# Differential heads: the inverse square root of the output norm moves from VectorE to GpSimd

## The chip, the cores and the metric

The kernel runs as one program on one core of a Trainium2 chip. The metric is the device time of an execution in microseconds (us); the time before is the median of three runs. A profile is one further execution with the hardware profiler on. Engines are named TensorE (PE in the rows; PEld its weight loads), VectorE (DVE), ScalarE (ACT), GpSimd (POOL) and SyncE (SP), which here issues the DMAs.

## What is computed

The model is two layers of a diffusion backbone over 1152 tokens (128 context, 1024 latent). The change lies in the second layer, in its eight differential-attention heads. For one head, with its own learned gate z and a scalar lam:

```python
s = jnp.einsum('bhiqd,bhikd->bhiqk', qb, k).astype(jnp.float32) * scale
p = jax.nn.softmax(s, axis=-1)
attn = p[:, :, 0] - lam * p[:, :, 1]
oc = jnp.einsum('bhqk,bhkv->bhqv', attn.astype(v.dtype), v)
...
oc = rmsnorm(oc, subln_g) * (1 - lam_init)   # per token, over the head's 128 values
out = jnp.concatenate([oc * jax.nn.silu(zc), od * jax.nn.silu(zd)], axis=-1) @ w_out
```

The norm needs one inverse square root for each token and head: 1152 for a head, which lie as 128 partitions by 9 columns.

## The kernel before

Tokens are cut into nine blocks of 128. Every large product is split into three half-precision products (high x high, high x low, low x high), so each operand lives as a pair (tile names ending in `hl`: high and low).

`odd` runs the eight heads one after the other (`diff_head`, heads 0 to 7 in the text), and after them eight window blocks of the other attention (`win_block`). For each block of queries a head computes two score maps of 1152 columns into `psS` (two PSUM buffers of three banks, so the next map waits until the last reader of the one before is done), VectorE takes the maximum (`sms`, L1290), ScalarE the exponential and its sum (L1292), VectorE combines the two maps into `p` (L1302 and L1303), ScalarE rounds `p` to half precision and GpSimd subtracts to get the low half (`phl`, L1304 and L1305), SyncE transposes it into `PT`, and about three blocks later TensorE multiplies it with V (`diff_pv`). ScalarE copies that result to `og` and sums its squares into `oss` (`diff_out`).

Between the scores TensorE works on the projections for the next heads, handed out in small pieces by a filler (`F.take`): `qk_block` for keys and queries and `v_block` for values. A projection's chunk of 384 columns goes to one of two PSUM buffers `psmm`; in `qk_block` it is read by ScalarE (`raw`, L1169) and VectorE (`q` times the cosine, L1175), then VectorE shuffles `raw` into `sw` (L1179), GpSimd multiplies by the sine and adds (L1180, L1181), and at the end ScalarE and GpSimd split `q` into `qhl` (L1187, L1188), which DMAs lay out as K or Q. TensorE can start the chunk after next only when both readers of a buffer are done. Weights are split into `whl` by ScalarE and VectorE (L322, L323).

When a head's last block is out, `diff_out` makes `oss` the mean square, `rsqrt` computes its inverse square root `orr` in integer and Newton steps, and `try_finish` multiplies `og` by it (L1249) and by the gate `zs` (L1250), splits the product into `gl` (ScalarE L509, GpSimd L510) and stores it. This falls some blocks into the next head's scores. In head 7 it falls into the first window block, where VectorE's masked reduction is L1378.

TensorE's order is that of the program. On the other engines a scheduler puts the instructions in order when the program is built, by priorities; the scores' and projections' readers have high priority, and the head's norm has not. Each engine then works its list strictly in order.

Of the kernel before, what the change touches and what calls it, by code (L numbers as in the profile page):

```python
# [10 lines left out]
F32 = mybir.dt.float32  # L11
F16 = mybir.dt.float16
I32 = mybir.dt.int32
AF = mybir.ActivationFunctionType
ALU = mybir.AluOpType
# [4 lines left out]
P = 128  # L20
# [3 lines left out]
NCH = T // P  # L24
KD = 8
WS = 64.0
IWS = 1.0 / WS
# [193 lines left out]
class Builder:  # L221
# [146 lines left out]
    def rsqrt(self, out, v, w, pool=None):  # L368

        nc = self.nc  # L370
        y = self.tl(pool or self.cm, [P, w], F32, f"rqy{w}")
        a = self.tl(pool or self.cm, [P, w], F32, f"rqa{w}")
        yi = y.bitcast(I32)
        nc.vector.tensor_scalar(yi, v.bitcast(I32), 1, None, ALU.logical_shift_right)
        nc.vector.tensor_scalar(yi, yi, -1, 0x5F3759DF, ALU.mult, ALU.add)
        for it in range(3):
            nc.vector.tensor_tensor(a, y, v, ALU.mult)
            nc.vector.scalar_tensor_tensor(a, a, -0.5, y, ALU.mult, ALU.mult)
            nc.vector.scalar_tensor_tensor(out if it == 2 else y, a, 1.5, y, ALU.add, ALU.mult)

    def rstd_stats(self, ssq, c0, c1, n):

        nc = self.nc
        m = (c1 - c0) // P
        st = self.pt("mm")
        for j in range(m):
            nc.tensor.matmul(st[:, j:j + 1], ssq[:, c0 + j * P:c0 + (j + 1) * P], self.ones[:, 0:1], start=True, stop=True)
        return self.rstd_diag(st[:, :m], m, n)
# [737 lines left out]
    def odd_setup(self):  # L1126
        nc, A = self.nc, self.A
        self.cosT = self.tl(self.rot, [P, TL], F32, "cos", 1)
        nc.sync.dma_start(self.cosT, A["cos"])
        self.sinT = self.tl(self.rot, [P, TL], F32, "sin", 1)  # L1130
        nc.sync.dma_start(self.sinT, A["sin"])
        self.mask = self.wt([P, 7, P], F32, tag="mask", bufs=1)
        nc.sync.dma_start(self.mask, A["mask"])

        lm = self.row("lam").rearrange("p (a b c) -> p a b c", a=2, b=2)
        pr = self.tl(self.rot, [P, 384], F32, "raw", 2)[:, :128].rearrange("p (a b) -> p a b", a=2)
        nc.vector.tensor_tensor(pr, lm[:, :, 0], lm[:, :, 1], ALU.mult)
        sm = self.wt([P, 4], F32, tag="lms", bufs=1)
        nc.vector.tensor_reduce(out=sm[:, 0:2], in_=pr, axis=AX.X, op=ALU.add)
        nc.scalar.activation(sm[:, 0:2], sm[:, 0:2], AF.Exp)  # L1140
        nc.vector.tensor_tensor(sm[:, 2:3], sm[:, 1:2], sm[:, 0:1], ALU.subtract)
        nc.vector.tensor_scalar(sm[:, 3:4], sm[:, 2:3], LAM_INIT, None, ALU.subtract)
        self.nlam = sm[:, 3:4]
        self.nsink = self.wt([P, 16], F32, tag="nsink", bufs=1)
        nc.vector.tensor_scalar(self.nsink, self.row("sink"), -1.0, None, ALU.mult)

# [92 lines left out]
    def try_finish(self, k):  # L1239

        if ("z", k) not in self.R or ("o", k) not in self.R:
            return
        zs, (og, r) = self.R.pop(("z", k)), self.R.pop(("o", k))
        nc = self.nc
        f = "p a b -> p (a b)"
        if r is None:
            nc.vector.scalar_tensor_tensor(og.rearrange(f), og.rearrange(f), 0.5 * IWS, zs.rearrange(f), ALU.mult, ALU.mult)
        else:
            nc.vector.tensor_tensor(og, og, r[:, :NCH].rearrange("p (a b) -> p a b", b=1).broadcast_to([P, NCH, P]), ALU.mult)  # L1249
            nc.vector.tensor_tensor(og.rearrange(f), og.rearrange(f), zs.rearrange(f), ALU.mult)  # L1250
        gl = self.wt([P, 2, NCH * P], F16, tag="gl", bufs=1)
        if k == 15:
            with self.tc.high_priority():
                self.split(gl, og.rearrange(f))
                t = self.ht()
                nc.sync.dma_start_transpose(t.rearrange("p a (c q) -> p (a c) q", q=P), gl.rearrange(f))
            self.gs[15] = t
            return
        self.split(gl, og.rearrange(f), nc.gpsimd)
        nc.sync.dma_start(self.go_dr[k], gl.rearrange(f))  # L1260
# [67 lines left out]
    def diff_out(self, po, h, b, sm, og, oss):  # L1328
        nc = self.nc
        nc.scalar.activation(og[:, b], po, AF.Copy, scale=sm[:, 6:7])  # L1330
        sq = self.wt([P, P], F32, tag="osq", bufs=1)
        nc.scalar.activation(sq, og[:, b], AF.Square, accum_out=oss[:, b:b + 1])
        if b < NCH - 1:
            return
        r = self.wt([P, 16], F32, tag="orr", bufs=2)
        nc.vector.tensor_scalar(oss[:, :NCH], oss[:, :NCH], 1.0 / 128, EPS, ALU.mult, ALU.add)
        self.rsqrt(r[:, :NCH], oss[:, :NCH], NCH)
        nc.vector.tensor_scalar(r[:, :NCH], r[:, :NCH], 0.5 * IWS, None, ALU.mult)
        del self.R["v", h]
        self.R["o", h] = (og, r)  # L1340
        self.try_finish(h)
# [310 lines left out]
```

## Time and profile before

| | |
|---|---|
| time before, median of 3 runs | 2256.24 us (2253.14 to 2256.71) |
| the profiled execution: its time, its span | 2259.94 us, 2258.0 us |
| mean granted TensorE clock | 0.957 of full speed |
| TensorE busy | 2025.2 us, 90% of the span |
| VectorE busy | 1470.4 us, 65% |
| ScalarE busy | 1223.2 us, 54% |
| GpSimd busy | 1060.9 us, 47% |
| chain that ended last, by engine | TensorE 42%, VectorE 20%, GpSimd 10%, ScalarE 9% |

The shares are means over the whole program. The last line follows the work that ended last backwards, step by step, to what released it. TensorE is busy for nine tenths of the span, so what an edit on another engine is worth shows only where TensorE waits, and these places must be looked at one by one. The eight heads lie between about 1040 and 1700 us.

### The profile page before, as it was taken

The page shows a single profiled execution, that of the slowest core. Times are in us where ns is not written, and L with a number is a line of the kernel's source. Part 1 is how long each engine was busy: PE and PEld are TensorE (multiplying, and loading weights), DVE is VectorE, ACT ScalarE, POOL GpSimd, SP SyncE. Part 2 cuts the span into 40 slices and gives each one's busy share as a digit, 9 for nine tenths or more (in the row PEclk, how much of TensorE's full clock was granted, in tenths as well). Part 3 has the DMA queues.
Part 4 walks back from the last instruction along what each step waited for, and adds up shares of the span by engine and source line. Part 5 has one row for each costly group of instructions (what it writes and reads, how often), then busy time and mean ns, then how long its engine had stood idle before and what let it go on. Part 6 is the DMA issues. An engine that isn't in the chain of part 4 may idle for free.

```text
span 2258.0 us, 49764 instructions
## 1 busy us (share of the span) xinstructions
PE 2025.2 (90%) x20258; PEld 1433.6 (63%) x20258; DVE 1470.4 (65%) x2722; ACT 1223.2 (54%) x2891; POOL 1060.9 (47%) x997
## 2 busy tenths in 40 slices
PE   5997788887989999998998999999988998998997
PEld 2654475564556655665776776776666777785566
DVE  5878988789586445575677677767765545451334
ACT  5575666566463312344655655665567867782321
POOL 1378677876675200044345345445446655661001
PEclk8998898998999999999999999999999999999999
DMA  7221513224557622035454554555456968899312
GB/s 281 72 79 48 152 58 102 75 94 122 183 202 217 164 99 88 31 132 118 95 122 108 117 123 113 112 126 115 109 123 134 175 146 160 163 176 210 139 47 84
DMA packets 435125, 283.10 MB, mean 125 GB/s; under 512 B 374448, under 2 KB 385232, under 8 KB 434896
## 3 DMA queue, kind: packets, MB, share of 16 engines
q1 hardware_dynamic: 433920, 279.34, 49.9%
q8 instruction: 158, 2.59, 0.5%
q10 hardware_dynamic: 976, 0.58, 0.1%
q14 instruction: 71, 0.58, 0.1%
HBM read 133.38 MB, written 29.05 MB: 72 GB/s over the span
## 4 chain that ended last, share of the span: by engine, by line
PE 42%; DVE 20%; POOL 10%; ACT 9%; issue 6%; DMA 5%; SPq 2%; POOLq 0%; ACTq 0%; DVEq 0%
PE psmm L329 8%; PE psmm L330 8%; PE psmm L331 8%; DVE sms L1290 3%; PE psS L1288 3%; DVE whl L323 3%; PE psm L329 2%; PE psm L330 2%; PE psm L331 2%; DVE p L1303 2%; DMA Q<-qhl 2%; ACT p L1380 1%; ACT p L1292 1%; DVE E L801 1%; PE psss L331 1%
## 5 line engine op out<-in xcount | busy, mean ns | idle before, releaser
L329 PE MATMUL psmm<-h,whl 128*128 128x384 f16 (+1 forms) x1104 | 370.2, 336 | 21.3 <-DVE q L1175 14.7
L330 PE MATMUL psmm<-h,whl 128*128 128x384 f16 (+1 forms) x1104 | 369.1, 335 | 2.3 <-DVE h L506 1.7
L331 PE MATMUL psmm<-h,whl 128*128 128x384 f16 (+1 forms) x1104 | 369.0, 335 | 0.0
L329 PE MATMUL psmm<-whl,h 128*128 128x128 f16 x1920 | 334.0, 220 | 10.1 <-DVE V L1211 10.1
L330 PE MATMUL psmm<-whl,h 128*128 128x128 f16 x1920 | 333.7, 220 | 0.0
L331 PE MATMUL psmm<-whl,h 128*128 128x128 f16 x1920 | 333.6, 220 | 0.0
L330 PEld LDWEIGHTS <-whl 128*128 128x128 f16 x2256 | 225.5, 100 | 167.9 <-issue 47.2
L331 PEld LDWEIGHTS <-whl 128*128 128x128 f16 x2256 | 225.2, 100 | 157.1 <-issue 18.9
L329 PEld LDWEIGHTS <-whl 128*128 128x128 f16 x2256 | 226.3, 100 | 147.3 <-issue 23.3
L1305 POOL TENSOR_TENSOR phl<-p,phl 128x1152 f16<-128x1152 f32 (+1 forms) x72 | 155.9, 2169 | 218.5 <-ACT phl L1304 218.5
L330 PEld LDWEIGHTS <-h 128*128 128x128 f16 x2520 | 246.7, 98 | 12.6 <-issue 10.8
L329 PEld LDWEIGHTS <-h 128*128 128x128 f16 x2520 | 246.8, 99 | 4.3 <-issue 2.6
L331 PEld LDWEIGHTS <-h 128*128 128x128 f16 x2520 | 246.6, 98 | 0.0
L323 DVE SCALAR_TENSOR_TENSOR whl<-w,whl 128x512 f16<-128x512 f32 x248 | 196.5, 811 | 67.0 <-ACT whl L322 66.0
L1290 DVE TENSOR_REDUCE sms<-psS 128x1 f32<-128x1152 f32 (+1 forms) x136 | 176.5, 1298 | 67.0 <-PE psS L1288 66.2
L1390 POOL TENSOR_TENSOR phl<-p,phl 128x1024 f16<-128x1024 f32 (+2 forms) x72 | 135.1, 1876 | 106.8 <-ACT phl L1389 85.8
L322 ACT ACTIVATE whl<-w 128x512 f16<-128x512 f32 x248 | 140.1, 609 | 78.2 <-PE psmm L331 42.2
L1288 PE MATMUL psS<-K,Q 128*128 128x512 f16 (+1 forms) x800 | 153.2, 328 | 25.1 <-DVE p L1303 19.3
L1180 POOL TENSOR_TENSOR sw<-sw,sin 128x384 f32<-128x384 f32 (+1 forms) x78 | 85.8, 1101 | 150.6 <-DVE sw L1179 127.2
L503 POOL TENSOR_TENSOR h<-mt,h 128x384 f16<-128x384 f32 (+2 forms) x32 | 28.9, 913 | 250.0 <-ACT h L502 250.0
L1288 PEld LDWEIGHTS <-Q 128*128 128x128 f16 x800 | 73.5, 99 | 94.2 <-DVE p L1303 21.9
L1292 ACT ACTIVATE psS<-psS,sms 128x1152 f32<-128x1152 f32 (+1 forms) x72 | 79.1, 1098 | 89.4 <-DVE sms L1290 88.9
(396 smaller groups left out, 5864.7 us busy)
## 6 DMA issues: line engine op xcount, KB each, us to landing
w<-in_wod SPq DMA_DIRECT2D x52, 512.0 KB, 4.0
w<-in_wev SPq DMA_DIRECT2D x40, 512.0 KB, 4.1
E<-csrow SPq DMA_DIRECT2D x36, 512.0 KB, 4.0
Q<-qhl SPq DMA_DIRECT2D x64, 288.0 KB, 4.3
go_dr<-gl SPq DMA_DIRECT2D x15, 576.0 KB, 3.9
wada<-in_w_ada SPq DMA_DIRECT2D x32, 256.0 KB, 5.8
o<-in_w_ada SPq DMA_DIRECT2D x16, 512.0 KB, 5.8
xT<-in_w_ada SPq DMA_DIRECT2D x16, 512.0 KB, 6.1
```

The lines of the kernel that those rows point to most:

```text
L322: nc.scalar.activation(hl[:, 0, a:e], w[:, a:e], AF.Copy if scale is None else AF.Identity, scale=sc)
L323: nc.vector.scalar_tensor_tensor(hl[:, 1, a:e], w[:, a:e], sc, hl[:, 0, a:e], ALU.mult, ALU.subtract)
L329: mm(out, ah, bh, start=start, stop=False)
L330: mm(out, ah, bl, start=False, stop=False)
L331: mm(out, al, bh, start=False, stop=stop)
L1180: nc.gpsimd.tensor_tensor(sw[:, o:], sw[:, o:], self.sinT[:, a:b], ALU.mult)
L1288: nc.tensor.matmul(sv[:, i, c0:c1], q[:, m, x, qs], k[:, m, o + c0:o + c1], start=x == 0, stop=x == 1)
L1290: nc.vector.tensor_reduce(out=sm[:, ms[0]:ms[-1] + 1], in_=sv, axis=AX.X, op=ALU.max, negate=True)
L1292: nc.scalar.activation(sv[:, i] if m else e, sv[:, i], AF.Exp, bias=sm[:, m:m + 1], accum_out=sm[:, 4 + m:5 + m])
L1303: nc.vector.scalar_tensor_tensor(p[0], p[1], sm[:, 2:3], p[0], ALU.mult, ALU.add)
L1305: nc.gpsimd.tensor_tensor(phl[:, w:2 * w], p[0], phl[:, :w], ALU.subtract)
L1390: nc.gpsimd.tensor_tensor(phl[:, 2 * w:4 * w], p, phl[:, :2 * w], ALU.subtract)
```

## The change

`rsqrt_pool` takes the place of `rsqrt` in `diff_out`. The two integer instructions that make the first guess stay on VectorE, as does the one that makes `oss` the mean square. The three Newton rounds run on GpSimd as thirteen `tensor_tensor` instructions on 128x9: one that multiplies the mean square by -0.5, then three rounds of four. Their constants -0.5 and 1.5 come from a tile `half`, filled once in `odd_setup`. The scale by `0.5 * IWS`, a VectorE instruction of its own before, moves into the product of `og` and `orr`.

```diff
+    def rsqrt_pool(self, out, v, w):
+        nc = self.nc
+        g = nc.gpsimd.tensor_tensor
+        y = self.tl(self.cm, [P, w], F32, f"rpy{w}")
+        a = self.tl(self.cm, [P, w], F32, f"rpa{w}")
+        yi = y.bitcast(I32)
+        nc.vector.tensor_scalar(yi, v.bitcast(I32), 1, None, ALU.logical_shift_right)
+        nc.vector.tensor_scalar(yi, yi, -1, 0x5F3759DF, ALU.mult, ALU.add)
+        g(v, v, self.half[:, 0, :w], ALU.mult)
+        for it in range(3):
+            g(a, y, y, ALU.mult)
+            g(a, a, v, ALU.mult)
+            g(a, a, self.half[:, 1, :w], ALU.add)
+            g(out if it == 2 else y, a, y, ALU.mult)
...
+        self.half = self.wt([P, 2, NCH], F32, tag="half", bufs=1)
+        for i, c in enumerate((-0.5, 1.5)):
+            nc.gpsimd.memset(self.half[:, i], c)
...
-            nc.vector.tensor_tensor(og, og, r[:, :NCH].rearrange("p (a b) -> p a b", b=1).broadcast_to([P, NCH, P]), ALU.mult)
+            nc.vector.scalar_tensor_tensor(og, og, 0.5 * IWS,
+                                           r[:, :NCH].rearrange("p (a b) -> p a b", b=1).broadcast_to([P, NCH, P]),
+                                           ALU.mult, ALU.mult)
...
-        self.rsqrt(r[:, :NCH], oss[:, :NCH], NCH)
-        nc.vector.tensor_scalar(r[:, :NCH], r[:, :NCH], 0.5 * IWS, None, ALU.mult)
+        self.rsqrt_pool(r[:, :NCH], oss[:, :NCH], NCH)
```

The scheduler makes new lists of it. TensorE's is unchanged. SyncE's differs in one place, in head 6, where a transpose of `phl` now stands behind the low half of a K store. Heads 0 to 5 change alike. A line of the new program from 380 on has a number 16 to 21 higher than its like in the old one.

VectorE at the end of head 0, before: after the reduction come the steps of the first two rounds (`rqy` and `rqa`), with a shuffle and `q` between them.

```order
L1290 TENSOR_REDUCE sms_13344<-psS_13346 128x1
L379 SCALAR_TENSOR_TENSOR rqy_1526_13246<-rqa_1527_13247,rqy_1526_13246 128x9
L377 TENSOR_TENSOR rqa_1527_13247<-rqy_1526_13246,oss_11999 128x9
L1179 STREAM_SHUFFLE sw_13368<-raw_13364 128x256
L1175 SCALAR_TENSOR_TENSOR q_1533_13297<-psmm_13305,cos_11480 128x256
...
L1338 TENSOR_SCALAR orr_13244<-orr_13244 128x9
L1249 TENSOR_TENSOR og_11998<-og_11998,orr_13244 128x1152
L1290 TENSOR_REDUCE sms_13344<-psS_13388 128x1
L1175 SCALAR_TENSOR_TENSOR q_1533_13297<-psmm_13372,cos_11480 128x384
L1179 STREAM_SHUFFLE sw_13409<-raw_13406 128x384
L1250 TENSOR_TENSOR og_11998<-og_11998,zs_12596 128x1152
```

The same place in the changed program:

```order
L1311 TENSOR_REDUCE sms_13350<-psS_13352 128x1
L1268 SCALAR_TENSOR_TENSOR og_12001<-og_12001,orr_13247 128x1152
L1194 SCALAR_TENSOR_TENSOR q_1534_13303<-psmm_13311,cos_11480 128x256
L1198 STREAM_SHUFFLE sw_13374<-raw_13370 128x256
L1271 TENSOR_TENSOR og_12001<-og_12001,zs_12599 128x1152
L1311 TENSOR_REDUCE sms_13350<-psS_13394 128x1
L1194 SCALAR_TENSOR_TENSOR q_1534_13303<-psmm_13378,cos_11480 128x384
L1198 STREAM_SHUFFLE sw_13415<-raw_13412 128x384
```

The product of `og` and `orr` now stands directly behind the reduction and ahead of `q` of 128x256, and `og` times `zs` ahead of the second reduction. On ScalarE `gl` stands accordingly ahead of the next `raw` and the next exponential, where it stood behind both.

GpSimd at the end of head 0, before:

```order
L1181 TENSOR_TENSOR q_1502_13053<-q_1502_13053,sw_13284 128x384
L1188 TENSOR_TENSOR qhl_13289<-q_1502_13053,qhl_13289 128x1280
L1305 TENSOR_TENSOR phl_13336<-p_13204,phl_13336 128x1152
L1180 TENSOR_TENSOR sw_13368<-sw_13368,sin_11482 128x256
L1181 TENSOR_TENSOR q_1533_13297<-q_1533_13297,sw_13368 128x256
L1180 TENSOR_TENSOR sw_13409<-sw_13409,sin_11482 128x384
L1181 TENSOR_TENSOR q_1533_13297<-q_1533_13297,sw_13409 128x384
L510 TENSOR_TENSOR gl_13262<-og_11998,gl_13262 128x1152
```

The same place in the changed program, from the third round on; the product with -0.5 and the first two rounds, nine rows, stand between `q` of 128x384 and the first row here:

```order
L392 TENSOR_TENSOR rpa_1528_13250<-rpy_1527_13249 128x9
L393 TENSOR_TENSOR rpa_1528_13250<-rpa_1528_13250,oss_12002 128x9
L394 TENSOR_TENSOR rpa_1528_13250<-rpa_1528_13250,half_11493 128x9
L1207 TENSOR_TENSOR qhl_13295<-q_1503_13056,qhl_13295 128x1280
L395 TENSOR_TENSOR orr_13247<-rpa_1528_13250,rpy_1527_13249 128x9
L1326 TENSOR_TENSOR phl_13342<-p_13207,phl_13342 128x1152
L1199 TENSOR_TENSOR sw_13374<-sw_13374,sin_11482 128x256
L1200 TENSOR_TENSOR q_1534_13303<-q_1534_13303,sw_13374 128x256
L526 TENSOR_TENSOR gl_13268<-og_12001,gl_13268 128x1152
```

Twelve of the thirteen instructions stand ahead of `qhl`, the last one, which writes `orr`, between `qhl` and `phl`; `gl` moved ahead of the `sw` and `q` of 128x384.

VectorE in head 7, in the first window block, before (the last removed instructions, then the masked reduction of the next block's scores, an ISA row):

```order
L1387 RECIPROCAL sms_21515<-sms_21515 128x2
L379 SCALAR_TENSOR_TENSOR orr_21489<-rqa_2288_21492,rqy_2287_21491 128x9
L1338 TENSOR_SCALAR orr_21489<-orr_21489 128x9
L1249 TENSOR_TENSOR og_20265<-og_20265,orr_21489 128x1152
L1378 ISA psS_2308_21599,sms_21597<-psS_2308_21599,mask_11484,nsink_11493 128x512
```

The same place in the changed program:

```order
L389 TENSOR_SCALAR rpy_2288_21515<-rpy_2288_21515 128x9
L1406 TENSOR_REDUCE sms_21542<-sms_21542 128x2
L1407 RECIPROCAL sms_21542<-sms_21542 128x2
L1268 SCALAR_TENSOR_TENSOR og_20286<-og_20286,orr_21513 128x1152
L1398 ISA psS_2309_21626,sms_21624<-psS_2309_21626,mask_11484,nsink_11496 128x512
```

The masked reduction keeps its place behind the `og` product, and that product now takes `orr` from GpSimd, whose thirteen instructions stand there in one piece, right ahead of a `phl` of 128x1024.

## Rows read from the trace of the kernel before

**Rows 1.** Who waited for whom, TensorE, whole run: total us, times, longest.

```profile
PE psmm L329 <- DVE q L1175: 14.7, 6, 2.4
```

**Rows 2.** Timeline, TensorE: start, duration, engine, line, [idle before, releaser].

```profile
1134.38 0.48 PE L329 MATMUL psmm<-h,whl 128*128 128x384 f16 x1 [2.44 <-DVE q L1175]
...
1143.53 1.15 PE L1288 MATMUL psS<-K,Q 128*128 128x512 f16 x6 [0.53 <-DVE p L1303]
...
1147.87 0.22 PE L1321 MATMUL psS<-V,PT 128*128 128x128 f16 x1 [0.34 <-ACT og L1330]
...
1158.06 0.22 PE L329 MATMUL psmm<-whl,h 128*128 128x128 f16 x1 [1.89 <-DVE V L1211]
...
1217.39 0.32 PE L329 MATMUL psmm<-h,whl 128*128 128x384 f16 x1 [2.45 <-DVE q L1175]
...
1490.03 0.22 PE L329 MATMUL psmm<-whl,h 128*128 128x128 f16 x1 [0.72 <-DVE V L1211]
```

**Rows 3.** Timeline, VectorE, end of head 0; the last row from head 7.

```profile
1129.05 1.35 DVE L1290 TENSOR_REDUCE sms<-psS 128x1 f32<-128x1152 f32 x1
...
1131.37 2.29 DVE L377 TENSOR_TENSOR rqa<-rqy,oss 128x9 f32<-128x9 f32 x1
...
1133.92 0.41 DVE L1175 SCALAR_TENSOR_TENSOR q<-psmm,cos 128x256 f32<-128x256 f32 x1
...
1136.31 1.36 DVE L1249 TENSOR_TENSOR og<-og,orr 128x1152 f32<-128x1152 f32 x1
...
1142.06 1.42 DVE L1303 SCALAR_TENSOR_TENSOR p<-psS,sms,p 128x1152 f32<-128x1152 f32 x1
...
1147.08 1.23 DVE L323 SCALAR_TENSOR_TENSOR whl<-w,whl 128x512 f16<-128x512 f32 x1
...
1700.42 0.17 DVE L377 TENSOR_TENSOR rqa<-rqy,oss 128x9 f32<-128x9 f32 x1
```

**Rows 4.** Timeline, GpSimd, end of head 0; the last row from head 7.

```profile
1126.30 1.01 POOL L1181 TENSOR_TENSOR q<-q,sw 128x384 f32<-128x384 f32 x1
1128.69 2.62 POOL L1188 TENSOR_TENSOR qhl<-q,qhl 128x1280 f16<-128x1280 f32 x1 [1.38 <-ACT qhl L1187]
...
1131.27 2.36 POOL L1305 TENSOR_TENSOR phl<-p,phl 128x1152 f16<-128x1152 f32 x1
...
1145.37 2.39 POOL L1305 TENSOR_TENSOR phl<-p,phl 128x1152 f16<-128x1152 f32 x1
...
1702.62 3.20 POOL L1390 TENSOR_TENSOR phl<-p,phl 128x1024 f16<-128x1024 f32 x1 [3.68 <-ACT phl L1389]
```

**Rows 5.** GpSimd groups by shape (count | busy us, mean ns), then two timeline rows.

```profile
L1305 POOL TENSOR_TENSOR phl<-p,phl 128x128 f16<-128x128 f32 x8 | 3.4, 427 | 7.8 <-ACT phl L1304 7.8
...
L944 POOL TENSOR_TENSOR ed<-V,rce 128x8 f32<-128x8 f32 x4 | 0.8, 205 | 10.6 <-DVE V L937 10.6
...
1134.09 0.72 POOL L1180 TENSOR_TENSOR sw<-sw,sin 128x256 f32<-128x256 f32 x1 [0.46 <-DVE sw L1179]
1134.89 0.74 POOL L1181 TENSOR_TENSOR q<-q,sw 128x256 f32<-128x256 f32 x1
```

**Rows 6.** Timeline, GpSimd and VectorE, first layer: handovers from one to the other.

```profile
143.28 0.67 POOL L510 TENSOR_TENSOR hb<-hst,hb 128x256 f16<-128x256 f32 x1
...
143.36 0.87 DVE L766 TENSOR_TENSOR xs<-x,dec 128x256 f32<-128x256 f32 x1 [1.14 <-POOL xshl L510]
...
154.48 0.43 DVE L766 TENSOR_TENSOR xs<-x,dec 128x256 f32<-128x256 f32 x1 [0.56 <-POOL xshl L510]
```

**Rows 7.** Timeline, ScalarE, end of head 0.

```profile
1141.18 1.16 ACT L509 ACTIVATE gl<-og 128x1152 f16<-128x1152 f32 x1 [0.89 <-DVE og L1250]
```

**Rows 8.** Timeline, TensorE, end of head 6.

```profile
1639.66 0.61 PE L1288 MATMUL psS<-K,Q 128*128 128x512 f16 x1 [5.11 <-DVE p L1303]
```

**Rows 9.** Timeline, head 7: VectorE's masked reduction; TensorE.

```profile
1703.75 0.75 DVE L1378 CUSTOM_DVE_ANT_0 psS<-psS,mask,nsink 128x512 f32<-128x512 f32 x1
...
1728.14 0.37 PE L1367 MATMUL psS<-K,Q 128*128 128x128 f16 x2 [5.75 <-DMA Q<-qhl]
```

## The prediction

> **What bounds the kernel now.** I read the waits of PE first, then, at the places where the removed instructions stand, VectorE, GpSimd and ScalarE in order of time. PE lost 14.7 us in six waits for VectorE's q L1175 [rows 1]: one in each of heads 0 to 5, and head 0 stands for them. There PE has four waits [rows 2]: 2.44 us for that q, then 0.53, 0.34 and 1.89 us, 5.2 in all, the last ending at 1158.06. After it the next wait is the next head's 2.45 us at 1217.39, 83 us after 1134.38. So what counts is when PE leaves 1158.06, and a delay before it costs nothing until the last three waits, 2.76 us together, are used up. In head 4 the last wait is 0.72 us instead of 1.89, at 1490.03 [rows 2], because PE came later; it left at the same place in the head's 83 us. So the end of that wait is set by the chain on VectorE, ScalarE and GpSimd, and PE has slack in front of it. Both must be followed.
>
> Why does VectorE let q wait? The third small instruction, L377 on 128x9, took 2.29 us (1131.37 to 1133.66) [rows 3], over the same stretch in which GpSimd ran the phl subtraction (1131.27 to 1133.63) [rows 4]. A 128x9 instruction takes 0.17 us when nothing stands in its way (at 1700.42) [rows 3]. So a VectorE instruction with two inputs in SBUF stands still while GpSimd works, if GpSimd began first. The reverse holds too: in head 7 phl 128x1024 took 3.20 us at 1702.62 [rows 4] because VectorE's og product had begun before it. This lock is what the change has to be judged by.
>
> **The change part by part.** Ten small VectorE instructions per head go (three rounds of three, and the scale by 0.5*IWS, now part of the og product, whose 1.36 us [rows 3] I leave as they are: the same elements, one more constant). Thirteen GpSimd instructions on 128x9 come; the two memsets of the constants run once, in the setup, at nothing beside the input loads; if uncovered they are two tiny instructions, under half a microsecond. Two things move with them. The og product now waits for GpSimd's last instruction, orr, and all that stands behind it on VectorE waits too, q 128x256 first. And qhl and phl on GpSimd stand behind the chain.
>
> **Price of a link.** No 128x9 instruction of GpSimd is in the trace; 128x8 takes 0.205 us [rows 5]. A GpSimd instruction that needs the one before it starts 0.08 us after its end (1134.09 + 0.72 to 1134.89) [rows 5]. So a link costs 0.28. Bounds: below, VectorE's own 0.17 with no gap; above, the 128x128 form, 0.43 [rows 5], with the gap, 0.51. I take 0.28, since 8 elements are next to 9.
>
> **Head 0, GpSimd.** It is free of q at 1127.31 (1126.30 + 1.01). Twelve links, of which the second does not need the first: 12 x 0.205 + 10 x 0.08 = 3.26, to 1130.6. Then qhl, 2.62, to 1133.2; orr, 0.2, to 1133.3; phl, 2.36, to 1135.65 [rows 4]. In the kernel before, qhl started at 1128.69, since it waits for ScalarE, so part of the chain fills idle time.
>
> **Head 0, who gets the lock.** When orr ends, phl is already queued behind it and VectorE has yet to see the semaphore. The trace has this race: at 143.28 GpSimd went straight on to hb, VectorE's product, released by the instruction before hb, was issued at 143.36 and took 0.87; where GpSimd went on to something tiny the same product took 0.43 [rows 6]. So phl wins, and og runs after it. L377 ended 0.03 after phl with 0.17 of its own, so the lock comes free about 0.14 before GpSimd's end: og runs from 1135.5 to 1136.9, and q 128x256 (0.41, starting 0.08 before og's end) ends at 1137.2. Before it ended at 1134.33 [rows 3]. **PE resumes 2.86 us later** and has 2.76 of slack: +0.1.
>
> **Head 0, the VectorE chain.** Its reduction ends at 1130.40 (1129.05 + 1.35); then it stands until 1135.5, and og is over at 1136.9, where before the removed instructions, with q among them, put og at 1136.31 to 1137.67 [rows 3]. Behind q come a shuffle (estimate 0.4, as q on as many elements), og times zs (as og, 1.36) and a reduction (1.35), each starting 0.08 before its forerunner ends: done at 1140.0. On ScalarE gl (1.16) [rows 7] starts when og times zs ends, at 1138.8, and now stands ahead of raw (estimate 0.4) and of the exponential (estimate 1.2, as gl on as many elements), which ends at 1141.5. The tiny sms instruction, with two SBUF inputs, then meets GpSimd's gl subtraction (as phl, 2.36), which now comes earlier: behind sw and q (0.72 and 0.74 [rows 5], from 1138.6) it runs from 1140.1 to 1142.5. So p starts at 1142.55 instead of 1142.06 [rows 3]: +0.5. But the whl of 1147.08 stood still for 0.54 of its 1.23, because phl ran until 1147.76 (1145.37 + 2.39) [rows 3, 4]; it now starts at 1147.6, and phl, which as before waits for gl and for p's copy on ScalarE, is over. The half microsecond is given back; the chain reaches 1158.06 as before. **Heads 0 to 5: +0.1 each, +0.6.** From here each 0.1 us on the chain is 0.1 us per head, both ways, because both paths end together.
>
> **Head 6.** Here the p for which PE waits 5.11 us at 1639.66 [rows 8] has og, og times zs and seven removed instructions shortly ahead of it on VectorE. In the new order the p before it stands behind the waiting og but og and the small ones are then gone from in front of this one. Bounds: 0, if that evens out, and +3.2, the price of head 7. I take +1.0.
>
> **Head 7.** GpSimd's first rounds start when VectorE's second integer instruction is done, about 1700.4 (L377 follows it at 1700.42). The twelve links left then give 12 x 0.205 + 11 x 0.08 = 3.3: orr ends at 1703.75. Then phl 128x1024 (2.13: 3.20 less the 1.07 it stood still) holds the lock until 1705.7; og to 1707.05; the masked reduction starts at 1707.0 instead of 1703.75 [rows 9]. That reduction's successors lead through a shuffle, q, qhl and the Q transfers to PE's 5.75 us wait at 1728.14 [rows 9], where nothing gives it back: **+3.2**.
>
> Sum: 0.6 + 1.0 + 3.2 = +4.8 us. The profiled execution's own time is 2259.94 (span 2258.0 and 1.94 around it), which would become 2264.7; it lies 3.7 above the median 2256.24, so the median becomes **2261.0**. A measurement of this kernel tells 0.2% (4.5 us) from no change; the forecast stands just beyond that.
>
> **The rivals.** *GpSimd is twice as slow.* If each link takes twice VectorE's 0.17, 0.34 and the gap 0.08, the chain in head 0 takes 12 x 0.34 + 10 x 0.08 = 4.9 instead of 3.26: +1.7 in each of heads 0 to 5 (10.2), head 6 +1.5, head 7 +4.9: +16.6, 2273. Against it: the 0.205 of rows 5. The Trainium skill, GPSIMD Engine Reference, section Engine selection, speaks for it and against the whole change: elementwise work with two inputs belongs on VectorE, GpSimd being about twice as slow. By that page's ratio the time would be this rival's; its figures are for 2048 elements, and no run here shows them.
>
> *Faster.* The links run back to back at 0.17: the chain takes 2.0 instead of 3.26, and with both paths of heads 0 to 5 earlier by 1.25 they gain 1.15 each (-6.9); head 6 0, head 7 +2.0: -4.9, 2251. It turns to a gain below about 0.22 a link. For it: the links are tiny and the engine's own. Against: each waits for the one before, and the 0.08 gap is in the trace.
>
> *Head 6 and 7 absorbed.* Their delays fall where later waits take them up: +0.6, 2257. For it: PE waits often after 1640. Against: those waits hang on the same chain.
>
> *VectorE wins the lock at orr.* Then og runs at 1133.35, phl behind it, q ends only 0.7 later; p comes about 0.6 earlier than in the forecast, though og times zs now meets phl: -0.5 in six heads, head 7 +1.5 instead of 3.2, head 6 +1: about -0.5, 2256. Against: rows 6.
>
> **Chances.** Forecast 0.50 (a link of 0.25 to 0.31 moves it from +1 to +9, so 0.27 slower and 0.23 the same), twice as slow 0.18, faster 0.12, absorbed 0.12, lock won 0.08. Faster by over 0.2%: 0.13; within: 0.40; slower: 0.47. The range holds all from the faster rival to the slow one's 2273: 2250 to 2273; the forecast's own is 2257 to 2265.
>
> **What would show it.** GpSimd's 128x9 rows at 0.2 us with 0.08 between; VectorE's og row in heads 0 to 5 taking about 3.5 us (the rest of phl and its own 1.36) after an idle of 3.0; PE's wait for q at about 5.3 instead of 2.44, and the 0.53, 0.34 and 1.89 gone; head 7's Q wait later by 3. I am wrong if og takes 1.36 there, if links cost over 0.35, or if some later wait in a head's 83 us opens up.

## The result, and the profile after

The changed kernel takes 2269.43 us, median of 12 runs (2264.0 to 2275.53), against 2256.0 for the kernel before (12 runs). The ratio is 1.0051, 95% interval 1.0040 to 1.0062: **+11.5 us** (9.0 to 14.0). Five later runs of it gave 1.0048 (1.0035 to 1.0062), +10.8. The forecast was slower, +4.8, 2261.0; the time lies in the range, but the sum is short by more than half.

The steps of the forecast in head 0 can be read in the new trace. First the chain on GpSimd in head 0, by its timeline:

```profile
1126.15 0.20 POOL L392 TENSOR_TENSOR rpa<-rpy 128x9 f32<-128x9 f32 x1
1126.43 0.20 POOL L393 TENSOR_TENSOR rpa<-rpa,oss 128x9 f32<-128x9 f32 x1
...
1129.12 2.61 POOL L1207 TENSOR_TENSOR qhl<-q,qhl 128x1280 f16<-128x1280 f32 x1
1131.69 0.20 POOL L395 TENSOR_TENSOR orr<-rpa,rpy 128x9 f32<-128x9 f32 x1
1131.85 2.36 POOL L1326 TENSOR_TENSOR phl<-p,phl 128x1152 f16<-128x1152 f32 x1
```

A link takes 0.20 us and the next starts 0.28 after it, as forecast from [rows 5]. The chain, then qhl, then orr, then phl stand in the order that was forecast. VectorE's timeline in the same place:

```profile
1127.75 1.35 DVE L1311 TENSOR_REDUCE sms<-psS 128x1 f32<-128x1152 f32 x1
1131.92 3.50 DVE L1268 SCALAR_TENSOR_TENSOR og<-og,orr 128x1152 f32<-128x1152 f32 x1 [2.83 <-POOL orr L395]
1135.35 0.41 DVE L1194 SCALAR_TENSOR_TENSOR q<-psmm,cos 128x256 f32<-128x256 f32 x1
```

The og product waits 2.83 us for orr and then takes 3.50 where it took 1.36 [rows 3], since phl (1131.85 to 1134.21) has the lock. The q eviction stands behind it. TensorE's waits in all, and its timeline at the four places that matter:

```profile
PE psmm L329 <- DVE q L1194: 31.0, 6, 5.2
```

```profile
1135.81 0.48 PE L329 MATMUL psmm<-h,whl 128*128 128x384 f16 x1 [5.16 <-DVE q L1194]
...
1630.77 2.08 PE L1309 MATMUL psS<-K,Q 128*128 128x512 f16 x6 [6.57 <-ACT og L1351]
...
1682.01 0.58 PE L1387 MATMUL psS<-K,Q 128*128 128x128 f16 x4 [5.05 <-DVE p L1324]
...
1735.24 0.37 PE L1387 MATMUL psS<-K,Q 128*128 128x128 f16 x2 [5.73 <-DMA Q<-qhl]
```

The waits for q go from 14.7 [rows 1] to 31.0 us, six times 5.2, and the waits of 0.53, 0.34 and 1.89 that followed in head 0 [rows 2] are gone: one long wait in place of four short ones in that head. The row at 1682.01 answers to nothing that the prediction read. It is the first score product of the window blocks; in the kernel before it waited 1.77 us for og, and the next wait was 0.95 us for p:

```profile
1678.87 0.38 PE L1367 MATMUL psS<-K,Q 128*128 128x128 f16 x4 [1.77 <-ACT og L1330]
...
1682.16 0.22 PE L1321 MATMUL pssm<-V,PT 128*128 128x128 f16 x1 [0.95 <-DVE p L1303]
```

To find the loss I cut both traces at the first instruction of the head's norm (`oss` on VectorE, 128x9), which stands in every kernel, and at TensorE's first long wait for Q behind head 7 [rows 9]. The stretches in us, each start being a row of the timeline (before 1125.29, 1619.59, 1696.56, 1728.14; after 1124.00, 1618.75, 1700.45, 1735.24):

| stretch | before | after | after, other run |
|---|---|---|---|
| oss of head 0 to oss of head 6 | 494.30 | 494.75 | 495.09 |
| oss of head 6 to oss of head 7 | 76.97 | 81.70 | 81.77 |
| oss of head 7 to the end of the Q wait | 31.58 | 34.79 | 34.83 |
| from there to the end of the span | 529.86 | 526.96 | 529.54 |

Heads 0 to 5 lose 0.5 to 0.8 us (forecast 0.6), head 7 loses 3.2 (forecast 3.2). Between head 6 and head 7 it is 4.7 to 4.8 where 1.0 was forecast. That is the surprise.

### The profile page after: what moved, and what is told of

Its sections match the earlier page's. It is cut to its first block, busy times and chain, and to the rows that moved or that the text cites. A ratio compares the mean times of both kernels' runs of the same rounds, so it can differ in the third digit from the quotient of the medians.

```text
span 2262.2 us, 49786 instructions
## 1 busy us (share of the span) xinstructions
PE 2020.7 (89%) x20258; PEld 1435.0 (63%) x20258; DVE 1445.2 (64%) x2642; ACT 1222.2 (54%) x2891; POOL 1082.5 (48%) x1103
## 5 line engine op out<-in xcount | busy, mean ns | idle before, releaser
L331 PEld LDWEIGHTS <-whl 128*128 128x128 f16 x2256 | 225.5, 100 | 157.6 <-issue 19.6
L323 DVE SCALAR_TENSOR_TENSOR whl<-w,whl 128x512 f16<-128x512 f32 x248 | 190.3, 786 | 64.6 <-ACT whl L322 63.7
L1325 ACT ACTIVATE phl<-p 128x1152 f16<-128x1152 f32 (+1 forms) x72 | 76.1, 1065 | 102.2 <-DVE p L1324 102.2
```

Of the source, the lines that this page charges most:

```text
L323: nc.vector.scalar_tensor_tensor(hl[:, 1, a:e], w[:, a:e], sc, hl[:, 0, a:e], ALU.mult, ALU.subtract)
L331: mm(out, al, bh, start=False, stop=stop)
L1325: nc.scalar.activation(phl[:, :w], p[0], AF.Copy)
```

## The experiments

**What lies behind the wait of 5.05.** The built programs show one more difference than the diff does. The pool of PSUM buffers decides at build time which of the two score buffers each `psS` tile gets. In the kernel before the 140 tiles of these buffers get them strictly in turn; in the changed kernel both maps of block 3 in head 7 get the same one, and from there on the two are exchanged:

```
first bank of tiles 125 to 133, before:  5 2 5 2 5 2 5 2 5
first bank of tiles 125 to 133, after:   5 2 5 2 2 5 2 5 2
```

So the second map of that block waits for the og that ScalarE reads from the first one's buffer (the 6.57 above), and the first window scores, whose banks are those of the first buffer, no longer follow the first map of the last block but the second one, which the last p still reads. All four kernels of the first group ran on one chip.

*The changed kernel again* (`r0_after_again`). Expected:

> The changed kernel once more, beside the three below on one chip. Both theories: about 1.005 of the kernel before (+11.5 us), PE's wait for q at 5.2 us in six heads, and the first window scores waiting 5.05 us for the last p of head 7.

Measured 1.0048 (1.0035 to 1.0062); the column "other run" above is its profile.

*The buffers in turn* (`e1_alternate`). The only edit:

```diff
+        if tag == "S":
+            self.turn = not getattr(self, "turn", False)
+            tag = "SA" if self.turn else "SB"
...
-                odps.enter_context(self.psum("dfps", S=2))
+                odps.enter_context(self.psum("dfps", SA=1, SB=1))
```

> The changed kernel with its two score buffers in PSUM given out strictly in turn, as they were in the kernel before; every engine's order of instructions is that of the changed kernel. Theory A (the 3.9 us lost between head 7's scores and the first window block come from the buffer that repeats in head 7, after which the first window scores lie in the buffer that the last p still reads): the wait of 5.05 splits again into about 1.8 and 1.0, the twelve matmuls behind it take about 2.1 instead of 3.8, and the wait of 6.57 for og in head 7's second block goes back to one for p; 4 to 5 us less than the changed kernel, a ratio of about 1.003. Rival (the late chain itself delays that place): the ratio stays at 1.005 and the wait of 5 us stays.

Measured 1.0023 (1.0010 to 1.0036), +5.2 us: 5.6 less than the changed kernel beside it. TensorE's timeline at the end of head 7:

```profile
1676.00 1.15 PE L1312 MATMUL psSB<-K,Q 128*128 128x512 f16 x6 [1.59 <-DVE p L1327]
...
1678.92 0.38 PE L1390 MATMUL psS<-K,Q 128*128 128x128 f16 x4 [1.77 <-ACT og L1354]
...
1682.20 0.22 PE L1345 MATMUL pssm<-V,PT 128*128 128x128 f16 x1 [0.94 <-DVE p L1327]
```

The wait of 5.05 is split into 1.77 and 0.94 again, with the projection's matmuls between them, as theory A said. The wait of 6.57 (it lies in block 3, not in the second block) is now one of 5.92 for p. Head 6 to head 7 takes 77.33 us. The loss has two parts, and the views by stretch show the second, first of the changed kernel, then of this one (length; TensorE, weight loads, VectorE, ScalarE, GpSimd busy, each with its number of instructions; then the granted clock, and what the DMAs moved):

```profile
1682.00:1686.30 4.30, 4.29 (x21) 2.39 (x22) 1.02 (x6) 2.54 (x8) 2.99 (x2) 0.55 0.76 191
```

```profile
1677.00:1681.30 4.30, 2.48 (x19) 1.39 (x16) 4.16 (x6) 3.20 (x8) 2.37 (x1) 1.00 0.12 24
```

Behind the wait of 5.05 the granted clock is 0.55, mostly the lower of its two levels (1.2 GHz); with waits of 1.77 and 0.94 it stays at 1.00 (2.4 GHz). The twelve matmuls of 384 columns take 3.8 us (1682.39 to 1686.22) instead of 2.1. So the exchange costs the 2.3 us of work that used to fill the wait, and 1.7 us of slow clock. The Trainium skill, TensorE: Matmul & The Clock Gate, Part 1, says that the engine's clock is halved when it has been idle and comes back with activity; the trace agrees at this wait, though not at every wait (see what stays open).

*The exchange alone, in the kernel before* (`e4_before_swap`, second group): the tiles in turn as above, except that the tile with number 129, counted from 0, does not turn.

```diff
+            self.nS = getattr(self, "nS", -1) + 1
+            if self.nS != 129:
+                self.turn = not getattr(self, "turn", False)
```

> The kernel before, with nothing changed but that the score buffer repeats once at the same place in head 7 where it repeats in the changed kernel, so that the two buffers are exchanged from there on; the Newton steps stay on VectorE. Theory A (the exchange costs 4 to 5 us by itself, whichever engine has the chain): 4 to 5.5 us slower than the kernel before, 1.002, the first window scores waiting about 5 us for p and the twelve matmuls behind it taking 3.8. Rival (the exchange hurts only with the late chain of GpSimd): 1.000.

Measured 1.0024 (1.0011 to 1.0037), +5.4 us, with the Newton steps on VectorE. TensorE's timeline, and the stretch behind the wait:

```profile
1682.71 0.58 PE L1372 MATMUL psS<-K,Q 128*128 128x128 f16 x4 [5.17 <-DVE p L1308]
```

```profile
1683.00:1687.30 4.30, 4.30 (x20) 2.22 (x19) 1.03 (x6) 2.13 (x8) 2.99 (x2) 0.52 0.65 170
```

The same wait and the same clock; head 6 to head 7 takes 82.49. Theory A holds in both directions: half of the changed kernel's loss is the exchange, and has nothing to do with which engine takes the Newton steps.

**Head 7's term.** *Buffers in turn, head 7 on VectorE* (`e2_alternate_head7_vector`):

```diff
+        if h == 7:
+            self.rsqrt(r[:, :NCH], oss[:, :NCH], NCH)
+        else:
+            self.rsqrt_pool(r[:, :NCH], oss[:, :NCH], NCH)
```

> As the run with buffers in turn, and head 7 has its Newton steps on VectorE as before. The prediction's term for head 7 (+3.2, carried to the wait for Q): 3.2 less than the run with buffers in turn, a ratio of about 1.0015, with the Q wait 3.2 us closer to head 7's first oss. Rival (the wait for Q takes the delay up): same time as that run.

Measured 1.0021 (1.0012 to 1.0030), where 1.0015 was expected: by the times no different from the run before it, though 3.2 us (0.0014) would not stand out between two such intervals. The timelines say more. The Q wait, first with head 7 on GpSimd (`e1_alternate`), then on VectorE:

```profile
1731.52 0.37 PE L1390 MATMUL psS<-K,Q 128*128 128x128 f16 x2 [5.52 <-DMA Q<-qhl]
```

```profile
1730.43 0.37 PE L1393 MATMUL psS<-K,Q 128*128 128x128 f16 x2 [5.79 <-DMA Q<-qhl]
```

From head 7's oss (1696.60 and 1698.32) that is 34.92 and 32.11. In the five profiles of this study with head 7 on GpSimd it is 34.79 to 34.92, in the seven with it on VectorE 31.28 to 32.11: means 34.86 and 31.64, +3.2 without overlap (e7 below, where head 7's products are cut up, is left out). From the Q wait to the end of the span the five take 526.96 to 530.79, the seven 526.38 to 530.17, means 529.5 and 528.8: on average nothing gives the delay back, though the spread of 4 us is wider than the term. I take head 7's 3.2 as shown to the Q wait, and as likely, not proved by the times, from there to the end.

*Head 7 alone* (`e10_head7_alone`, third group). Heads 0 to 6 keep `self.rsqrt`, with the factor fused into the product as in the change; buffers in turn.

> Heads 0 to 6 as before but with the factor 0.5 IWS fused into the product (one instruction of 0.17 less a head); head 7 alone has its Newton steps on GpSimd; buffers in turn. By the prediction's terms: the six heads 0 to -1.2, head 7 +3.2 to the wait for Q; 1.0 to 3.2 us slower than before, 1.0005 to 1.0014. If head 7's delay is taken up by the later waits for Q's transfers: the same as before, with the first Q wait 3.2 later and the last of the window stage's no later than 1.

Measured 1.0066 (1.0050 to 1.0082), +14.9 us: a miss. Head 7 gives its 3.3 (34.89 to the Q wait), but oss of head 0 to head 6 takes 500.83 us, 6.5 more than before. VectorE's and TensorE's timelines in head 0:

```profile
1141.16 1.35 DVE L1274 TENSOR_TENSOR og<-og,zs 128x1152 f32<-128x1152 f32 x1
1142.42 0.55 DVE L1197 SCALAR_TENSOR_TENSOR q<-psmm,cos 128x384 f32<-128x384 f32 x1
```

```profile
1160.56 0.22 PE L332 MATMUL psmm<-whl,h 128*128 128x128 f16 x1 [2.04 <-DVE V L1233]
```

Taking one instruction of 0.17 us out of the list let the scheduler put og times zs ahead of the eviction of q (384 columns), in heads 0 to 5; in the kernel before it stood behind. That eviction starts 14.63 us behind the head's oss instead of 13.57. But the delay is made up: TensorE's wait for V ends 32.8 us behind oss in both kernels (at 1158.06 [rows 2] and at 1160.56). The loss lies in the clock, as the stretch from oss of head 0 to oss of head 6 shows, first of the kernel before, then of this one:

```profile
1125.29:1619.59 494.30, 461.68 (x5349) 355.32 (x5348) 358.40 (x542) 296.06 (x585) 234.56 (x144) 0.98 0.52 116
```

```profile
1127.79:1628.62 500.83, 468.63 (x5349) 361.98 (x5348) 358.85 (x535) 296.17 (x585) 228.14 (x144) 0.97 0.52 115
```

The same 5349 matmuls keep TensorE busy 6.95 us longer, and it is idle 0.4 less. In heads 0, 1, 3 and 5 the clock falls once more, behind the wait for V, and the head is 1.6 us longer; in heads 2 and 4, with the same order and the same wait of 2.03 to 2.04, it does not, and they take the 83.0 us of before. The 4.3 us behind that wait, before in head 0, here in head 0 and here in head 2:

```profile
1158.06:1162.36 4.30, 4.30 (x66) 3.82 (x66) 2.89 (x5) 1.69 (x3) 0.50 (x1) 1.00 1.02 200
```

```profile
1160.56:1164.86 4.30, 4.30 (x46) 4.23 (x46) 2.89 (x5) 1.69 (x3) 0.50 (x1) 0.60 1.00 189
1329.86:1334.16 4.30, 4.30 (x67) 3.83 (x67) 2.89 (x5) 1.69 (x3) 0.46 (x1) 1.00 1.02 192
```

So the edit that should save a fifth of a microsecond a head costs 1.1 on average. That the new order moves TensorE's waits is shown (in head 0 the one for p ends 27.7 us behind oss instead of 18.2); that this is what lets the clock fall a second time is likely, but was not tried by itself.

**Where the og products stand.** In the kernel as changed og blocks q. *Both products behind block 3's p* (`e3_alternate_og_late`, first group), on top of buffers in turn:

```diff
+            with self.tc.issue_after(self.q0):
+                fn()
```

Here `q0` is VectorE's p of block 3, and `fn` issues the two products, ahead of block 4.

> As the run with buffers in turn, and in heads 0 to 6 the product og times orr and the one with zs are issued on VectorE behind block 3's p instead of ahead of the q eviction. Theory (what costs PE its 5.2 us a head is only that og stands and waits ahead of q on VectorE): PE's wait for q goes from 5.2 to under 1 in six heads; if half to all of it stays gained, 15 to 31 us less than the run with buffers in turn, well below the kernel before. Rival (VectorE's chain of max and p has no room, and the waits for p that vanished come back): the sum of PE's waits in a head stays near 5.2 and the time within 3 us of the run with buffers in turn.

Measured 1.0000 (0.9990 to 1.0011): 5 us under `e1_alternate`, 15 to 31 were hoped for. The timelines of VectorE, then of GpSimd and TensorE, behind block 3's p in head 0:

```profile
1135.27 1.46 DVE L1271 SCALAR_TENSOR_TENSOR og<-og,orr 128x1152 f32<-128x1152 f32 x1
...
1137.92 3.21 DVE L1274 TENSOR_TENSOR og<-og,zs 128x1152 f32<-128x1152 f32 x1
...
1141.53 1.34 DVE L1316 TENSOR_REDUCE sms<-psSB 128x1 f32<-128x1152 f32 x1
```

```profile
1137.54 2.38 POOL L1331 TENSOR_TENSOR phl<-p,phl 128x1152 f16<-128x1152 f32 x1
...
1144.52 0.26 PE L1347 MATMUL psSA<-V,PT 128*128 128x128 f16 x1 [4.33 <-ACT og L1356]
```

The wait for q is gone, as the theory said. The same og product takes 1.46 us here, with no phl beside it, where it took 3.50. But now the product with zs meets phl and takes 3.21, the maximum of a map that was ready waits behind it, and TensorE waits 4.33 for what follows. There is something of the theory and of the rival in this: the wait left q, and 4.33 of its 5.2 us came back elsewhere. The Trainium skill, SBUF — State Buffer, section SBUF: two separate sides, calls the port that VectorE and GpSimd share an exclusive lock, held for a whole instruction by whichever starts first; 1.46 against 3.50 and 3.21 agree.

*Both products behind block 4's p*, with the steps on VectorE (`e5_before_og_later`) and on GpSimd in heads 0 to 6 (`e6_og_later_head7_vector`), and *in nine pieces* (`e7_one_pass`), second group:

> The kernel before, Newton steps on VectorE, with the two og products of heads 0 to 6 issued behind block 4's p instead of ahead of block 3's second max. Theory (place of the products on VectorE is what costs PE its 5.2 us a head, in both kernels): PE's waits in a head fall by 1 to 4 us of 5.2, six heads, 6 to 24 us faster than before. Rival (waits come back as in the run with the products behind block 3's p): within 5 us of before.

> As that run, but the Newton steps of heads 0 to 6 on GpSimd (head 7's on VectorE), buffers in turn. Theory: with the products out of the way, the chain on GpSimd has time, and VectorE is rid of nine small instructions: 1 to 2 us a head below the run with the chain on VectorE, so 6 to 12 us less than that. Rival (the chain's place no longer matters once the products stand later): same time.

> As the run before it, with the two 128x1152 products of all heads made into nine 128x128 instructions that multiply by orr and by zs at once (the factor 0.5 IWS goes into the first operation on oss). By 0.41 for 128x256 and 0.56 for 128x384 in the rows, 0.26 each with some overlap: 2.0 us instead of 2.7 to 4.9 a head, and the lock is held in short pieces: 0 to 2 us a head less, 0 to 12 us in all. Rival (nine instructions cost more in issue than the second pass): up to 5 us more.

```diff
+            for b in range(NCH):
+                nc.vector.scalar_tensor_tensor(og[:, b], og[:, b], r[:, b:b + 1], zs[:, b], ALU.mult, ALU.mult)
```

Measured: e5 1.0086 (1.0072 to 1.0100), e6 0.9999 (0.9989 to 1.0009), e7 1.0049 (1.0034 to 1.0065). The chain on GpSimd is worth 19.6 us here, e5 against e6, more than the 6 to 12 expected, but neither beats the kernel before: e5, hoped to be 6 to 24 us faster, is 19 slower. TensorE's timeline in head 0, e5 and then e6:

```profile
1135.68 0.32 PE L332 MATMUL psmm<-h,whl 128*128 128x384 f16 x1 [2.45 <-DVE q L1178]
...
1161.28 0.27 PE L332 MATMUL psmm<-whl,h 128*128 128x128 f16 x1 [4.92 <-DVE V L1214]
```

```profile
1154.71 0.27 PE L332 MATMUL psmm<-whl,h 128*128 128x128 f16 x1 [5.36 <-DVE V L1233]
```

With the steps on VectorE the old wait for q stays and a long one for V comes on top; on GpSimd only the latter is left. In e7 the price of a piece, expected at 0.26, is 754 ns in the mean, waits for the lock included. VectorE's and GpSimd's timelines:

```profile
1149.20 6.15 DVE L1272 SCALAR_TENSOR_TENSOR og<-og,orr,zs 128x128 f32<-128x128 f32 x7
...
1156.54 0.60 DVE L1272 SCALAR_TENSOR_TENSOR og<-og,orr,zs 128x128 f32<-128x128 f32 x2
```

```profile
1150.16 2.40 POOL L1210 TENSOR_TENSOR qhl<-q,qhl 128x1152 f16<-128x1152 f32 x1 [1.27 <-ACT qhl L1209]
1152.52 2.41 POOL L1329 TENSOR_TENSOR phl<-p,phl 128x1152 f16<-128x1152 f32 x1
```

Two undisturbed pieces take 0.60. The seven take 6.15, with both of GpSimd's long instructions inside: between pieces GpSimd gets the lock, twice here, where one long instruction gives it away at most once, at its start.

**A place that pays.** From e3: let the product with zs wait until the second maximum of block 4 and its eviction are issued (`e8_og_split_gpsimd`; head 7 on VectorE, buffers in turn), and the same with all steps on VectorE (`e9_og_split_vector`), third group.

```diff
+            self.late = {4: first, 5: second}
...
+            with self.tc.issue_after(self.at):
+                fn()
```

`first` is og times orr, issued ahead of block 4 and behind block 3's p; `second` is the product with zs, issued ahead of block 5 and behind block 4's second maximum.

> Newton steps of heads 0 to 6 on GpSimd, head 7's on VectorE, score buffers in turn; on VectorE the product og times orr stands behind block 3's p, the one with zs behind block 4's second max and its eviction, where phl has let go of SBUF. Theory (what PE waits for in the run with both products behind block 3's p is the max that stands behind the product with zs, held 3.2 us by phl): that wait of 4.3 falls to 1 or less, 2 to 3.5 us a head, so 12 to 20 us under the kernel before. Rival (the waits move on to V's eviction as in the run with the products behind block 4's p): within 5 us of before.

> The same places for the two products, but the Newton steps of all heads on VectorE as before. Theory (the nine small instructions on VectorE now cost their own time, since nothing else holds PE there; twelve instructions took from 1127.38 to 1136.27 with waits): 1 to 2.5 us a head more than with the steps on GpSimd, 6 to 15 us above that run. Rival (the place of the chain does not matter): within 4 us of that run.

Measured: e8 **0.9964** (0.9949 to 0.9979), 8.1 us under the kernel before; e9 1.0069 (1.0053 to 1.0084), 15.6 us over it. The profiled run of e8 gains 14.8 up to the Q wait, but its 12 runs spread from 2241.5 to 2256.2 (the five fastest with a mean granted clock of 0.961 or 0.962, the others with 0.957 to 0.959), so I hold to the interval: less than the 12 to 20 hoped for, but the only kernel here that beats both. VectorE's and TensorE's timelines of e8, and of e9 the instruction and the wait that it has more:

```profile
1138.12 1.46 DVE L1370 SCALAR_TENSOR_TENSOR og<-og,orr 128x1152 f32<-128x1152 f32 x1
...
1143.14 1.35 DVE L1312 TENSOR_REDUCE sms<-psSB 128x1 f32<-128x1152 f32 x1
...
1146.15 2.08 DVE L1271 TENSOR_TENSOR og<-og,zs 128x1152 f32<-128x1152 f32 x1
```

```profile
1143.97 0.22 PE L1347 MATMUL psSA<-V,PT 128*128 128x128 f16 x1 [0.93 <-ACT og L1356]
```

```profile
1131.75 2.29 DVE L380 TENSOR_TENSOR rqa<-rqy,oss 128x9 f32<-128x9 f32 x1
...
1134.76 0.48 PE L332 MATMUL psmm<-h,whl 128*128 128x384 f16 x1 [2.45 <-DVE q L1178]
```

The wait of 4.33 is 0.93. In e9 a Newton step of VectorE still meets phl, takes 2.29 as in the kernel before [rows 3], and TensorE waits its 2.45 for q again. From oss of head 0 to oss of head 6, e8 takes 480.59 and e9 506.60 us: 4.3 a head, and 23.7 us by the times, more than the 1 to 2.5 a head expected. The views of these stretches, e8 and then e9, say where it lies:

```profile
1125.68:1606.27 480.59, 456.01 (x5349) 352.79 (x5348) 334.61 (x481) 295.46 (x585) 254.69 (x222) 0.99 0.55 120
```

```profile
1125.67:1632.27 506.60, 466.60 (x5349) 359.88 (x5348) 362.00 (x535) 295.43 (x585) 238.54 (x144) 0.97 0.51 113
```

In e9 TensorE is idle 15.4 us more, nearly all of it the six waits of 2.45 for q, and the same 5349 matmuls keep it busy 10.6 us longer, at a lower clock. In head 0 the granted clock behind the q wait is 0.65 (1134.76 to 1139.06); in e8, where TensorE does not wait at that place, it is 1.00.

## Why the prediction was right or wrong

The direction was right and so was the mechanism in head 0 and head 7. One term was missing, another left out the clock, and that the time still lies in the range is in part luck.

- **Price of a link**, 0.28: right (0.20 and a start every 0.28 us). The rival at twice the price falls: the Trainium skill's ratio of about two for two inputs (GPSIMD Engine Reference, section Engine selection) does not show at 128x9, where 0.20 stands against VectorE's 0.17. The faster rival, links back to back, falls too; so does the one in which later waits take up heads 6 and 7, as far as the Q wait.
- **Who gets the lock**: phl, as forecast; og 3.50 long in heads 0 to 5. The rival in which VectorE wins falls.
- **Heads 0 to 5**, +0.6: the sum is right (+0.5 to +0.8 in two profiles, +0.4 with the buffers in turn), but partly by luck. TensorE's wait for q went to 5.2 (forecast 5.3), and the three waits behind it were used up but for some 0.3 us for V in heads 1 and 4. Yet no head loses 0.1: from oss to oss heads 0, 1, 3 and 4 take 82.82 to 82.85 us, 0.1 to 0.2 less than before, and heads 2 and 5 take 83.54 and 79.84, 0.5 to 0.6 more. The sum has no term for the clock. In the changed kernel TensorE is idle 0.9 us less over these six heads than before (the view of before stands with e10), but busy 1.4 longer with the same matmuls, and behind the same q wait of 5.17 us the granted clock is 0.72 in head 1 and 0.50 in head 2 (views below).
- **Head 7**, +3.2: right to the tenth at the Q wait. The times cannot separate it from nothing (e1 against e2, where 3.2 was expected).
- **Head 6**, +1.0: this is the step that failed; the traces show 4.7 between the oss of head 6 and that of head 7. With the buffers in turn head 6 costs 0.4, less than forecast; the other 4.4 (81.70 less 77.33), or 5.4 to 5.6 by the times, are the exchange of the score buffers. This is the later wait that opens up, which the prediction named as a sign of being wrong. The prediction took the program of before for given where the change did not touch it, and compared the order of instructions, which does not show the buffers. The kernel that the forecast describes is `e1_alternate`: +5.2 (2.3 to 8.1) for a forecast of +4.8, with the luck of heads 0 to 5 in it.
- Sum: 0.5 + 0.4 + 3.2 in the profiles' stretches, and 5.4 to 5.6 for the exchange, give 9.5 to 9.7 of the 10.8 to 11.5 measured. The rest lies inside the intervals.

The views for heads 0 to 5: the changed kernel from oss of head 0 to oss of head 6, then the 5.4 us behind the q wait in its heads 1 and 2.

```profile
1124.00:1618.75 494.75, 463.04 (x5349) 356.04 (x5348) 338.74 (x481) 295.50 (x585) 249.26 (x222) 0.97 0.54 116
```

```profile
1218.63:1224.03 5.40, 5.39 (x42) 3.40 (x42) 4.86 (x9) 2.74 (x4) 4.92 (x4) 0.72 0.71 139
1301.49:1306.89 5.40, 5.40 (x34) 3.85 (x34) 4.85 (x9) 2.74 (x4) 4.94 (x4) 0.50 0.71 139
```

**What stays open.** Why the pool repeats a buffer in the changed kernel was not tried. And why the granted clock falls behind one wait and not behind its like: in the kernel before it is 0.62 behind the q wait of 2.44 in head 0 (1134.38 to 1138.70) and 1.00 behind that of 2.45 in head 1 (1217.39 to 1221.69).

## What to carry to other kernels

When the chain of small instructions is moved off an engine, what waits for its result has to be moved too: here the kernel with the product ahead of the readers that TensorE waits for is 5 us slower than the one before, and the one with it behind them (head 7 left out) 8 us faster. After an edit compare, beside the order of instructions, which buffer each tile of a pool got, at every place where one stage hands over to the next. An exclusive port shared by two engines was not made cheaper here by cutting an instruction into pieces: put the instruction where the other engine's long one is not. And to price a change beside a busy TensorE, compare its busy time over the same matmuls too: idle time alone does not show what the clock took.

## What the runs showed of the hardware that was not expected

A wait of 5 us costs more than itself: behind it the granted clock was 0.52 to 0.55, and 2.1 us of matmuls took 3.8; two waits of 1.77 and 0.94 us, with work between them, left it at 1.00. Shorter waits can cost the same: behind the one of 2.04 for V in e10 it was 0.60 in head 0, and 1.00 behind its like in head 2; four such stretches made that kernel 6.5 us slower. Nine VectorE instructions of 0.30 us let GpSimd take the shared lock twice, and seven of them took 6.15 us.
